# Transposes in a PSUM bank of their own, attention and mLSTM products in the other three: a hybrid decoder block on one core

## The chip, the cores and the metric

The kernel runs on one core of one Trainium2 chip. The metric is the device time of one execution in microseconds (us); the median of several runs counts. Names of engines in the profile: PE is TensorE's matmuls, PEld its weight loads, DVE is VectorE, ACT ScalarE, POOL GpSimd, SP SyncE, which issues all DMAs of this kernel. "L204" is line 204 of the kernel's file.

## What is computed

One decoder block over 2048 tokens of 1024 features, in float32. The reference, cut to what matters here:

```python
h = modulate(rms_norm(x, g_pre_mix), shift_m, scale_m)
proj = h @ w_in        # q,k,v | mLSTM q,k,v,o | pre-gates i,f | branch gates
q_a, k_a = rope(q_a, positions), rope(k_a, positions)      # 8 q heads, 2 kv heads of 64
y_a = sliding_window_attention(q_a, k_a, v_a, sinks)       # blocks of 128, window 128
qk_m = silu(causal_depthwise_conv(concat(q_m, k_m)))
h_m = mlstm_chunkwise(q_m, k_m, v_m, i_pre, f_pre)         # 4 heads of 128
y_m = sigmoid(o_m) * head_layer_norm(h_m)
merged = sigmoid(g_a) * (y_a @ w_branch_attn) + sigmoid(g_m) * (y_m @ w_branch_mlstm)
x = x + gate_m * rms_norm(merged @ w_out, g_post_mix)
h2 = modulate(rms_norm(x, g_pre_ffn), shift_f, scale_f)
ff = (silu(h2 @ w_ffn_gate) * (h2 @ w_ffn_up)) @ w_ffn_down   # 2816 wide
x = x + gate_f * rms_norm(ff, g_post_ffn)
```

## The kernel before

**Precision and products.** A float32 operand is split into two float32r halves, hi (a copy on ACT) and lo (the difference, on DVE: L259 and L260 for weights, L1356 and L1357 for the FFN), and a product is three matmuls: hi by hi, hi by lo, lo by hi. All of them go through mm (L200 to L204); all transposes go through transpose (L206 to L209) and are matmuls with an identity matrix. Where a weight pair allows it, four products of half-size blocks are made from seven (pair_parts).

**Blocks.** Tokens are worked on in four blocks of 512; two make a superblock (function superblock), and the FFN follows with program2 over the same two halves. In a superblock, b0 and b1 are its blocks, and the items come in this order: q and kv projections of b0, attend(b0), the v projection of the mLSTM (vm) of b0, then kv, q and vm of b1, attend(b1), then 14 pairs of column groups for both blocks (in_pair), then the outputs of both.

**PSUM.** There are eight banks, each a tile of 128 x 512 float32. ps_acc has four under the tag acc, for projections (acc_tile). ps_mix has four under the tag mix (mix_tile), for everything else: the transposes of h (hprep, L515), q (q_stream, L767), k (k_stream, L794), gates (gates, L846 and L877), mLSTM k (chunk_state, L1015) and mLSTM output (chunk_out, L1086), the score, probability and output tiles of attention (L921, L954, L966), the mLSTM's products (L1032, L1048, L1059), the transposes of h_combine for the FFN (L1398), and those FFN products that don't go to an acc tile (L1481, L1756).

**SBUF tiles that matter here.** tx is a tag with nine buffers of 128 x 512 float32 (L103). A projected kv or q tile is copied from its acc bank into a tx tile (L806, L781), the rotary writes a second one (L754 to L761), and both are kept until the transposed halves, which overwrite them, have been written to at_d in memory (L773, L799 to L801). at() reads them back for attention (L903 to L908). v of the mLSTM takes a tx tile as well (L826, L827).

**Order.** The projections are a list of parts that run2 goes through. Beside them run generators, the streams: each yields a time after which it is due again, counted by a sum of planned PE time (now), and tick() after every few matmuls takes up what is due. finish(...) runs streams until the ones that it names have ended. That gives the order in which the code asks for tiles and writes instructions down. From it the tile framework makes each engine's own order: it goes by readiness in its own reckoning of time, hands out the buffers of a tag, and sets the semaphores. So an engine's order in the trace differs from the code's in many places. The delays that matter here are L_ROPE and L_ROPEK (after which a rotated q or k tile is transposed), L_HT (between two h tiles), L_SOFT, L_PT and L_PV (in attention) and L_GATE and L_SCAN (in the gates).

**The parts that the change touches.** Transposes of h: one(k) in hprep makes four 128 x 128 transposes into one tile, which ACT reads twice (L518, L520) and DVE makes the lo half (L521); eight such tiles a block. q_stream: four transposes a tile, read by ACT (L771) and DVE (L772). k_stream: one transpose, read by ACT (L797) and DVE (L798), two writes to at_d. Attention on one block of 128 queries: four score tiles (for two halves of the heads and two kv groups), copied by ACT (L931) and masked by DVE (L933); softmax on DVE, ACT and POOL (L938 to L950); two tiles of transposed probabilities (L956, read by L959 and L963); one output tile of four matmuls (L969, read by L972 and L973). Two attention streams alternate, for even and odd blocks.

Of the kernel before, what the change touches and what calls it, by code (L numbers as in the profile page):

```python
# [10 lines left out]
F32 = mybir.dt.float32  # L11
# [8 lines left out]
P = 128  # L20
# [51 lines left out]
def decoder_block(ctx: ExitStack, tc: tile.TileContext, a: dict, out: bass.AP, dbg=None):  # L72
# [24 lines left out]
    def acc_tile():  # L97
        return ps_acc.tile([P, 512], F32, tag="acc", name=nm("acc"))

    def mix_tile():  # L100
        return ps_mix.tile([P, 512], F32, tag="mix", name=nm("mix"))

# [383 lines left out]
    def hprep(b, first=False):  # L486
# [25 lines left out]
        def one(k):  # L512
            name = f"{k // 4 + 1}{odd + 1}"
            hi, lo = (hc_part(name, i)[:, k % 4, :] for i in range(2))
            ps = mix_tile()  # L515
            for t in range(NT):
                transpose(ps[:, t * P:(t + 1) * P], xs[t][:, k * P:(k + 1) * P])
            A.activation(hi, ps, AF.Identity, scale=s1[:, k:k + 1], bias=sh1[:, k:k + 1])  # L518
            v = vs[k // 4][:, k % 4, :]
            A.activation(v, ps, AF.Identity, scale=s1[:, k:k + 1], bias=sh1[:, k:k + 1])  # L520
            (G if first else V).tensor_tensor(lo, v, hi.bitcast(F32), op=ALU.subtract)  # L521
# [214 lines left out]
    def superblock(sb):  # L736
        b0, b1 = 2 * sb, 2 * sb + 1
        R = {}
# [25 lines left out]
        def q_stream(b, t, yz):  # L764
            yield L_ROPE
            y, z = yz
            pt = mix_tile()  # L767
            for j in range(GQ):
                transpose(pt[:, j * P:(j + 1) * P], y[:, j * P:(j + 1) * P])
            hi, lo = z.bitcast(F32R), y.bitcast(F32R)  # L770
            A.activation(hi, pt, AF.Copy, scale=HD ** -0.5)  # L771
            V.scalar_tensor_tensor(lo, pt, HD ** -0.5, hi.bitcast(F32), op0=ALU.mult, op1=ALU.subtract)  # L772
            for i, q in enumerate((hi, lo)):  # L773
                nc.sync.dma_start(at_d[b * NT + t][:, i * 512:(i + 1) * 512], q.bitcast(F32))
# [16 lines left out]
        def k_stream(n, yz):  # L791
            yield L_ROPEK
            y, z = yz
            pt = mix_tile()  # L794
            transpose(pt[:, :P], y)
            kk = z[:, P:3 * P].bitcast(F32R).rearrange("p (i k) -> p i k", i=2)
            A.copy(kk[:, 0, :], pt[:, :P])  # L797
            V.tensor_tensor(kk[:, 1, :], pt[:, :P], kk[:, 0, :].bitcast(F32), op=ALU.subtract)  # L798
            for n_, u in ((n, 1), (n + 1, 0)):  # L799
                if n_ < S // P:  # L800
                    nc.sync.dma_start(at_d[n_][:, AT_K:AT_V].rearrange("p (i u k) -> p i u k", i=2, u=2)[:, :, u, :], kk.bitcast(F32))  # L801
# [30 lines left out]
        def gates(b):  # L832
# [12 lines left out]
            yield L_GATE  # L845
            pg = mix_tile()  # L846
            for t in range(NT):
# [28 lines left out]
            yield L_SCAN  # L876
            pc_ = mix_tile()  # L877
            for t in range(NT):
# [122 lines left out]
        def chunk_state(c):  # L1001
# [12 lines left out]
            yield L_LOAD  # L1014
            pk = mix_tile()  # L1015
            for hh in range(MH):
# [25 lines left out]
        def chunk_out(c):  # L1042
# [42 lines left out]
            yield L_LN  # L1085
            py = mix_tile()  # L1086
            for hh in range(MH):
# [290 lines left out]
    def h_combine(b2, rows, quarters, sums):  # L1378
# [14 lines left out]
        for k in range(4):  # L1393
            xk = xn
            v = {}
            for j, (half, i) in enumerate(QUADS):
                kk = k + 4 * half
                ps = mix_tile()  # L1398
                for t in range(4):
# [66 lines left out]
    def pair_parts(w, c0, done, new, spare, bank):  # L1466

        raw = raw_cols2(w, c0)
        R = {}

        def make(i, prep):
            B = PROD[i][1]

            def mms(wt):
# [13 lines left out]
                combine(i, ps, R, new, done)  # L1488
            return Part(raw, prep, mms, weave=bank is not mix_tile, ahead=4)

# [69 lines left out]
    def gate_up(b2):  # L1560
        late = None
        for p in range(NP):
# [26 lines left out]

            gp, up = (list(pair_parts(w, p * 256, done, unit, unit, mix_tile)) for w, done in ((wg, done_g), (wu, done_u)))  # L1590
            load, sums = down_weights(p)
# [35 lines left out]
    def down(b2):  # L1627
# [105 lines left out]
        def make(raw, i, p, j):  # L1733
# [16 lines left out]
            def mms(ab):  # L1750
                if p == 0:
                    for t in range(NT):
                        if i == 0:
                            R[t]["X"] = acc_tile()
                        if i not in IN_X:
                            R[t]["Y"] = mix_tile()  # L1756
                if hold:
# [112 lines left out]
```

## Time and profile before

| | us |
|---|---|
| median of 3 runs | 2711.97 |
| lowest and highest run | 2708.91, 2712.32 |
| the profiled execution | 2716.59 |
| its span, first to last instruction | 2714.9 |
| PE idle in the span (2714.9 - 2639.2 busy) | 75.7 |

How to read it: all times are in us from the span's start, unless marked ns. A row of groups is line, engine, operation, out<-in by the program's names without buffer numbers, shapes, count, then busy us and mean ns of one, then idle time of the engine just before them with what ended it. A row of the timeline is start, length, engine, line, operation, names, shapes and count, with an idle time in brackets. A row of one tile or one line has the shortest, median and longest duration in ns and the first and last start. Matmuls are pipelined, so the records of one after another overlap, and PE's throughput is read from starts or from busy time over a count.

### The profile page before, as it was taken

How to read it: one execution, taken by the hardware profiler on the slowest of the kernel's cores; microseconds unless marked ns; L12 is line 12 of the kernel's file. 1: busy time of each engine (PE TensorE's matmuls, PEld its weight loads, DVE VectorE, ACT ScalarE, POOL GpSimd, SP SyncE). 2: the span in 40 equal slices, each digit the busy share in tenths (PEclk: the TensorE clock that was granted, in tenths of full speed). 3: DMA queues.
4: the chain of work that ended last, by engine and by line, in shares of the span. 5: the costliest groups of instructions: out<-in, count | busy, mean ns of one | idle time of the engine just before them, and what ended most of it. 6: DMA issues, size and time to landing. Idle time of an engine off the chain costs nothing.

```text
span 2714.9 us, 35793 instructions
## 1 busy us (share of the span) xinstructions
PE 2639.2 (97%) x12310; PEld 2138.9 (79%) x12310; DVE 1986.2 (73%) x3906; ACT 1299.8 (48%) x2558; POOL 148.2 (5%) x189
## 2 busy tenths in 40 slices
PE   6989999999998999999999999999999999999998
PEld 4867788888885678888887888888877888888886
DVE  7968788778695778876687777776677676766456
ACT  5556544444755564444563443335554333333444
POOL 2010001100101000110000000000000000000000
PEclk8999999999998999999999999999999999999999
DMA  7654355897574544678765564436675232324566
GB/s 249 206 184 157 128 172 179 269 340 248 196 235 147 196 138 138 213 231 291 251 224 198 175 201 152 155 113 213 215 271 188 97 117 86 113 97 144 186 210 217
DMA packets 353639, 511.90 MB, mean 189 GB/s; under 512 B 25120, under 2 KB 213660, under 8 KB 348208
## 3 DMA queue, kind: packets, MB, share of 16 engines
q1 hardware_dynamic: 353456, 509.61, 56.9%
q8 instruction: 97, 1.59, 0.2%
q14 instruction: 86, 0.70, 0.1%
HBM read 357.12 MB, written 144.02 MB: 185 GB/s over the span
## 4 chain that ended last, share of the span: by engine, by line
PE 85%; DVE 7%; DMA 4%; ACT 2%; issue 1%; POOL 0%; SPq 0%; DVEq 0%; ACTq 0%; POOLq 0%
PE acc L204 61%; PE mix L204 22%; PE mix L209 2%; DVE hl L1357 1%; DVE tm L428 1%; DMA raw<-as_d 1%; ACT tm L946 1%; ACT hl L1356 1%; DMA raw<-in_w_in_dram 1%; DMA at_d<-tx 0%; DMA big<-in_x_dram 0%; DVE wlo L260 0%; DMA tx<-in_w_ada_dram 0%; DVE w L1667 0%; DMA at<-at_d 0%
## 5 line engine op out<-in xcount | busy, mean ns | idle before, releaser
L204 PE MATMUL acc<-big,hl 128*128 128x512 f32 x3936 | 940.8, 394 | 4.3 <-ACT tx L827 1.8
L204 PEld LDWEIGHTS acc<-big,hl 128*128 128x128 f32 x3936 | 733.3, 188 | 172.5 <-issue 13.8
L1356 ACT CAST hl<-raw 128x512 fp32r<-128x512 f32 x732 | 440.1, 621 | 493.4 <-PE acc L204 222.2
L1357 DVE TENSOR_TENSOR hl<-raw,hl 128x512 fp32r<-128x512 f32 x732 | 496.3, 694 | 194.8 <-ACT hl L1356 194.0
L204 PE MATMUL acc<-whi,big 128*128 128x512 f32 (+1 forms) x1280 | 379.3, 377 | 10.8 <-ACT big L518 8.4
L204 PEld LDWEIGHTS acc<-whi,big 128*128 128x128 f32 x1280 | 236.2, 192 | 52.4 <-ACT big L518 8.5
L204 PE MATMUL mix<-big,hl 128*128 128x512 f32 x1056 | 263.9, 391 | 1.7 <-ACT hl L1356 1.1
L204 PE MATMUL acc<-wlo,big 128*128 128x512 f32 (+1 forms) x640 | 241.2, 379 | 6.4 <-DVE wlo L260 6.4
L204 PE MATMUL acc<-hl,hl 128*128 128x512 f32 x1008 | 237.4, 393 | 5.1 <-DVE hl L1357 3.4
L204 PEld LDWEIGHTS mix<-big,hl 128*128 128x128 f32 x1056 | 197.9, 188 | 45.9 <-ACT hl L1356 1.9
L204 PEld LDWEIGHTS acc<-hl,hl 128*128 128x128 f32 x1008 | 187.0, 188 | 50.9 <-DVE hl L1357 8.8
L204 PE MATMUL mix<-hl,hl 128*128 128x512 f32 x792 | 182.7, 391 | 1.3 <-DVE hl L1357 0.9
L204 PEld LDWEIGHTS mix<-hl,hl 128*128 128x128 f32 x792 | 147.9, 188 | 35.3 <-DVE hl L1357 3.1
L204 PE MATMUL acc<-big,whi 128*128 128x512 f32 x512 | 157.4, 393 | 0.0
L260 DVE TENSOR_TENSOR wlo<-raw,whi 128x1024 fp32r<-128x1024 f32 (+1 forms) x96 | 109.0, 1137 | 65.5 <-ACT whi L259 59.8
L259 ACT CAST whi<-raw 128x1024 fp32r<-128x1024 f32 (+1 forms) x96 | 94.3, 983 | 123.8 <-PE acc L204 110.4
L204 PEld LDWEIGHTS acc<-wlo,big 128*128 128x128 f32 x640 | 123.7, 193 | 28.3 <-DVE wlo L260 8.6
L475 POOL TENSOR_TENSOR rs<-ms,nhalf 128x1 f32<-128x1 f32 (+1 forms) x56 | 42.6, 772 | 1617.5 <-DVE ms L473 1610.5
L204 PE MATMUL mix<-hcT4h,hl 128*128 128x512 f32 x352 | 117.7, 395 | 0.7 <-ACT hl L1356 0.7
L204 PE MATMUL acc<-hcT2h,hl 128*128 128x512 f32 x352 | 117.6, 394 | 0.0
L204 PEld LDWEIGHTS acc<-big,whi 128*128 128x128 f32 x512 | 95.4, 188 | 19.2
L204 PE MATMUL acc<-big,wlo 128*128 128x512 f32 x256 | 97.7, 393 | 0.0
(330 smaller groups left out, 3491.5 us busy)
## 6 DMA issues: line engine op xcount, KB each, us to landing
raw<-in_w_in_dram SPq DMA_DIRECT2D x48, 1024.0 KB
as_d<-w SPq DMA_DIRECT2D x154, 256.0 KB
raw<-as_d SPq DMA_DIRECT2D x70, 512.0 KB
raw<-in_w_ffn_gate_dram SPq DMA_DIRECT2D x22, 1024.0 KB
raw<-in_w_ffn_up_dram SPq DMA_DIRECT2D x22, 1024.0 KB
raw<-ws_d SPq DMA_DIRECT2D x40, 512.0 KB
y_d<-tm SPq DMA_DIRECT2D x64, 256.0 KB
tx<-in_w_ada_dram SPq DMA_DIRECT2D x64, 256.0 KB
```

The source lines that it names most:

```text
L204: T.matmul(o, lhsT=lhsT, rhs=rhs, start=start, stop=stop, skip_group_check=resumed)
L209: T.transpose(o, i, ident[:k, :k])
L259: A.copy(hv, src)
L260: V.tensor_tensor(lv, src, hv.bitcast(F32), op=ALU.subtract)
L428: V.scalar_tensor_tensor(acc, raw[:, k, :], c_, acc, op0=ALU.mult, op1=ALU.add)
L475: G.tensor_tensor(r[:, :n], ms[:, :n], nhalf[:, :n], op=ALU.pow)
L946: A.activation(sc[g][:, j, :], sc[g][:, j, :], AF.Exp, bias=nm_[:, hd:hd + 1], accum_out=sums[:, hd:hd + 1])
L1356: A.copy(v(hi), src)
L1357: V.tensor_tensor(v(lo), src, v(hi).bitcast(F32), op=ALU.subtract)
```

## The change

mix_tile keeps the pool's tag mix, now with three buffers. A new tr_tile has one buffer under the tag tr, and any_tile takes the two in turn: three mix tiles, then one tr tile. The transposes of h, q, k, the gates (twice), mLSTM k and mLSTM output ask for tr_tile; attention's tiles (its transposed probabilities too) and the mLSTM's products still ask for mix_tile; h_combine's transposes and the FFN's products ask for any_tile. The pool has four banks as before. In pair_parts the test for weaving streams into the matmuls now compares with any_tile, so that the FFN's parts stay unwoven.

```diff
--- before.py
+++ after.py
@@ -97,8 +97,17 @@
     def acc_tile():
         return ps_acc.tile([P, 512], F32, tag="acc", name=nm("acc"))
 
+    turn = [0]
+
     def mix_tile():
-        return ps_mix.tile([P, 512], F32, tag="mix", name=nm("mix"))
+        return ps_mix.tile([P, 512], F32, tag="mix", name=nm("mix"), bufs=3)
+
+    def tr_tile():
+        return ps_mix.tile([P, 512], F32, tag="tr", name=nm("tr"), bufs=1)
+
+    def any_tile():
+        turn[0] = (turn[0] + 1) % 4
+        return mix_tile() if turn[0] else tr_tile()
 
     def tx(shape, dtype=F32):
         return tpool.tile(shape, dtype, tag="tx", name=nm("tx"), bufs=9)
@@ -512,7 +521,7 @@
         def one(k):
             name = f"{k // 4 + 1}{odd + 1}"
             hi, lo = (hc_part(name, i)[:, k % 4, :] for i in range(2))
-            ps = mix_tile()
+            ps = tr_tile()
             for t in range(NT):
                 transpose(ps[:, t * P:(t + 1) * P], xs[t][:, k * P:(k + 1) * P])
             A.activation(hi, ps, AF.Identity, scale=s1[:, k:k + 1], bias=sh1[:, k:k + 1])
@@ -764,7 +773,7 @@
         def q_stream(b, t, yz):
             yield L_ROPE
             y, z = yz
-            pt = mix_tile()
+            pt = tr_tile()
             for j in range(GQ):
                 transpose(pt[:, j * P:(j + 1) * P], y[:, j * P:(j + 1) * P])
             hi, lo = z.bitcast(F32R), y.bitcast(F32R)
@@ -791,7 +800,7 @@
         def k_stream(n, yz):
             yield L_ROPEK
             y, z = yz
-            pt = mix_tile()
+            pt = tr_tile()
             transpose(pt[:, :P], y)
             kk = z[:, P:3 * P].bitcast(F32R).rearrange("p (i k) -> p i k", i=2)
             A.copy(kk[:, 0, :], pt[:, :P])
@@ -843,7 +852,7 @@
             V.tensor_tensor(l_, l_, d_, op=ALU.add)
             V.scalar_tensor_tensor(fv, fv, 0.0, l_, op0=ALU.min, op1=ALU.subtract)
             yield L_GATE
-            pg = mix_tile()
+            pg = tr_tile()
             for t in range(NT):
                 transpose(pg[:36, t * P:(t + 1) * P], gt[:, t, :])
             lf = tm([MH, TB])
@@ -874,7 +883,7 @@
             mp = small.tile([P, MH, 8], F32, tag="mp", name=nm("mp"), bufs=2)
             nc.sync.dma_start(mp, sm_d.unsqueeze(0).to_broadcast([P, MH, 8]))
             yield L_SCAN
-            pc_ = mix_tile()
+            pc_ = tr_tile()
             for t in range(NT):
                 transpose(pc_[:, t * 68:(t + 1) * 68], rw[:, t * P:(t + 1) * P])
             cl = small.tile([P, NT, 3, 4], F32, tag="cl", name=nm("cl"), bufs=2)
@@ -1012,7 +1021,7 @@
             vc = vmt[n_ % 2]
             nc.sync.dma_start(vc[:, :, :MD], vm_d[b][:, t, :].rearrange("p (h d) -> p h d", h=MH))
             yield L_LOAD
-            pk = mix_tile()
+            pk = tr_tile()
             for hh in range(MH):
                 transpose(pk[:, hh * P:(hh + 1) * P], km[:, hh, :])
             kw = tm([P, MH, P])
@@ -1083,7 +1092,7 @@
                 o = pn[hh // 2][:, (hh % 2) * 129:(hh % 2) * 129 + P]
                 A.activation(ym[:, hh, :], o, AF.Identity, scale=cf[:, hh:hh + 1], bias=vr[:, hh:hh + 1])
             yield L_LN
-            py = mix_tile()
+            py = tr_tile()
             for hh in range(MH):
                 transpose(py[:, hh * P:(hh + 1) * P], ym[:, hh, :])
             V.tensor_tensor(om, py.rearrange("p (h t) -> p h t", h=MH), om, op=ALU.mult)
@@ -1395,7 +1404,7 @@
             v = {}
             for j, (half, i) in enumerate(QUADS):
                 kk = k + 4 * half
-                ps = mix_tile()
+                ps = any_tile()
                 for t in range(4):
                     transpose(ps[:, t * P:(t + 1) * P], xk[j][:, t, :])
                 q = quarters()
@@ -1486,7 +1495,7 @@
                     mm(ps, l[1], r[0], False, kk == 3, True)
                     yield
                 combine(i, ps, R, new, done)
-            return Part(raw, prep, mms, weave=bank is not mix_tile, ahead=4)
+            return Part(raw, prep, mms, weave=bank is not any_tile, ahead=4)
 
         for i, prep in enumerate(a_operands(raw, spare)):
             yield make(i, prep)
@@ -1587,7 +1596,7 @@
                 for n, t_ in (("S1", s1_), ("S3", a_["21"]), ("S2", s2_), ("S4", s4_)):
                     nc.sync.dma_start(as_d[b2][:, IDX[n], p, :], t_)
 
-            gp, up = (list(pair_parts(w, p * 256, done, unit, unit, mix_tile)) for w, done in ((wg, done_g), (wu, done_u)))
+            gp, up = (list(pair_parts(w, p * 256, done, unit, unit, any_tile)) for w, done in ((wg, done_g), (wu, done_u)))
             load, sums = down_weights(p)
             if F.get("late") is not None and p == 0:
                 def a_step():
@@ -1753,7 +1762,7 @@
                         if i == 0:
                             R[t]["X"] = acc_tile()
                         if i not in IN_X:
-                            R[t]["Y"] = mix_tile()
+                            R[t]["Y"] = any_tile()
                 if hold:
                     F.setdefault("held", []).append((p, ab))
                     if p == NP - 1:
```

## The prediction

> **What bounds the kernel now.** I read the page first, then PE's busy time by stretches, then who read which tile in the stretches where PE is not full.
>
> ```profile
> span 2714.9 us, 35793 instructions
> ## 1 busy us (share of the span) xinstructions
> PE 2639.2 (97%) x12310; PEld 2138.9 (79%) x12310; DVE 1986.2 (73%) x3906; ACT 1299.8 (48%) x2558; POOL 148.2 (5%) x189
> ```
>
> PE is busy for 97% of the span, so all that any change of waits can win lies in 76 us. The view of windows says where they are (columns: stretch and length, then busy us and count of PE, PEld, DVE, ACT and POOL, then PE's granted clock, DMA share, GB/s):
>
> ```profile
> 158.50:184.50 26.00, 19.14 (x97) 9.61 (x96) 13.38 (x38) 14.67 (x53) 4.68 (x5) 0.87 0.39 119
> 838.00:866.40 28.40, 18.98 (x88) 9.82 (x84) 13.77 (x39) 14.56 (x52) 4.67 (x5) 0.70 0.35 113
> 210.00:310.00 100.00, 100.00 (x476) 72.53 (x474) 78.38 (x171) 63.12 (x163) 9.36 (x8) 1.00 0.39 126
> 890.00:935.00 45.00, 40.50 (x199) 31.72 (x200) 35.19 (x84) 31.58 (x85) 4.16 (x4) 0.96 0.55 178
> 66.00:120.00 54.00, 49.41 (x311) 44.12 (x310) 50.47 (x126) 33.94 (x59) 1.17 (x2) 0.98 0.65 209
> 745.00:800.00 55.00, 49.73 (x310) 43.89 (x311) 48.95 (x131) 28.80 (x52) 0.00 (x0) 0.97 0.75 248
> 1440.00:1840.00 400.00, 400.00 (x1757) 328.18 (x1756) 299.17 (x489) 154.04 (x280) 2.16 (x4) 1.00 0.51 163
> ```
>
> In two stretches, 158.5 to 184.5 and 838 to 866.4, PE is a quarter to a third idle although no other engine is near full. Attention woven into projection matmuls doesn't do that by itself: from 210 to 310 it leaves PE no idle time. The two stretches are the same place of the program in the two superblocks: the q projection of the second block has ended and its v projection should run. What it lacks is shown by ACT's reads and writes of the tx tiles from 120 to 200, and by the last step of the rotary on DVE (L761) in two windows:
>
> ```profile
> L781 ACT COPY tx<-acc x4: 585/586/592, 153.2 to 187.0; 128x512 f32<-128x512 f32 x4
> L797 ACT CAST tx<-mix x4: 265/269/272, 182.4 to 186.3; 128x128 fp32r<-128x128 f32 x4
> L771 ACT ACTIVATE tx<-mix x4: 585/591/597, 188.1 to 195.8; 128x512 fp32r<-128x512 f32 x4
> ...
>   DMA at_d<-tx: 1.0, 2
> ```
> ```profile
> 120.00:137.00 17.00, 0.86 (x4) 0.97 0.59 187
> 137.00:181.80 44.80, 0.00 (x0) 0.93 0.44 134
> ```
>
> The four rotated key tiles were ready by 137, but their transposes were read (L797) from 182.4 on, 45 us later. Until then they kept their tx tiles (two for each key tile, of nine in all), so of the four copies of q out of the acc banks (L781) one ran at 153.2 and the others by 187.0, behind a DMA of those tx tiles to at_d. Three acc banks stood full, v had one, and PE was left with attention alone. In the second superblock the last q copies and the key reads fall together again, at 863.6 to 868.3:
>
> ```profile
> L781 ACT COPY tx<-acc x4: 592/593/607, 827.0 to 868.3; 128x512 f32<-128x512 f32 x4
> L797 ACT CAST tx<-mix x4: 265/266/272, 863.6 to 868.2; 128x128 fp32r<-128x128 f32 x4
> ```
>
> Why were the key transposes late? All tiles of the tag mix come in the order in which the code asks for them, and the code asks for the tiles of some attention blocks just ahead of the key tile's. Those wait for softmax; the key tile waits behind them for no reason of its own. That order is my reading of these rows, and the forecast hangs on it.
>
> **The change part by part.** *Keys, queries, gates, h, k and y of the mLSTM go to a bank of their own.* For keys this takes the queue behind attention away. Ahead of them in the new queue stand only gate transposes, which don't wait for attention. So the key transposes run near 137, their two at_d writes a tile go to SP's queue some 45 us earlier, the tx tiles come free, q is copied out as it ends, and v runs while attention is woven in. The gain is each stretch less the time that its PE work needs. The work, by form, for the first stretch, then for the second, then the transposes of both:
>
> ```profile
> L204 PE MATMUL mix<-tm,at 128*64 128x512 f32 x22 | 9.9, 800 | 0.0
> L204 PE MATMUL mix<-at 64*128 64x256 f32 x48 | 4.4, 289 | 2.7 <-DMA at<-at_d 2.7
> ```
> ```profile
> L204 PE MATMUL mix<-tm,at 128*64 128x512 f32 x20 | 9.7, 898 | 0.0
> L204 PE MATMUL mix<-at 64*128 64x256 f32 x48 | 5.7, 415 | 3.7 <-DMA at<-at_d 2.4 <-DVE tm L933 1.3
> ```
> ```profile
> 158.50:184.50 26.00, 3.78 (x19) 2.30 (x19) 0.87 0.39 119
> 838.00:866.40 28.40, 4.29 (x19) 2.65 (x19) 0.70 0.35 113
> ```
>
> What is left of 97 and 88 instructions is 8 and 1 projection matmuls. The prices come from other places: the whole run's group of the 128*64 matmuls, and single rows of PE's timeline.
>
> ```profile
> L204 PE MATMUL mix<-tm,at 128*64 128x512 f32 x124 | 51.7, 695 | 0.0
> ```
> ```profile
> 74.92 0.60 PE L209 MATMUL mix<-ident,tx 128*128 128x128 f32 x4
> ...
> 108.87 0.28 PE L204 MATMUL acc<-wlo,big 128*128 128x264 f32 x1
> ...
> 149.48 1.07 PE L204 MATMUL mix<-tm,at 128*64 128x512 f32 x2
> ...
> 753.05 0.60 PE L209 MATMUL mix<-ident,tx 128*128 128x128 f32 x4
> ...
> 784.20 0.37 PE L204 MATMUL acc<-whi,big 128*128 128x264 f32 x1
> ...
> 836.71 1.94 PE L204 MATMUL mix<-tm,at 128*64 128x512 f32 x8
> ```
>
> One 128*64 matmul takes 0.42 on the whole (51.7/124), 0.24 at best (1.94/8) and 0.53 in a lone pair (1.07/2). A score matmul takes 0.09 (4.4/48), a transpose 0.13 (0.60/4 less an end that overlaps), a projection matmul 0.23 (400/1757). First stretch: 22x0.42 + 48x0.09 + 19x0.13 + 8x0.23 = 17.9 of 26.0, so 8.1 to win; with 0.24 it is 12.0, with 0.53 it is 5.7. Second: 20x0.42 + 4.3 + 2.5 + 0.2 = 15.4 of 28.4, so 13.0; bounds 16.6 and 10.8. Together 21.1, between 16.5 and 28.6; I take the whole run's pace since woven attention has that pace. Later, 890 to 935 holds 4.5 us of PE idle in which late v copies have a part; I take 1.5 of it, between 0 and 4.5.
>
> *The price: one bank for transposes.* A tile's next transposes now wait until the last tile is read. The nearest rows are those of the start of the first superblock, 65.9 to 91.7, ACT's two reads of an h tile in that window, and DVE's read of the q tile whose transposes began at 74.92:
>
> ```profile
> L518 ACT ACTIVATE big<-mix,sh,s 128x512 fp32r<-128x512 f32 x8 | 6.4, 799 | 3.7 <-PE mix L209 3.7
> L520 ACT ACTIVATE big<-mix,sh,s 128x512 f32<-128x512 f32 x8 | 6.4, 796 | 0.0
> ```
> ```profile
> 80.91 0.69 DVE L772 SCALAR_TENSOR_TENSOR tx<-mix,tx 128x512 fp32r<-128x512 f32 x1
> ```
>
> Alone an h tile takes 0.6 + 0.8 + 0.8 = 2.2, a q tile 0.6 + 0.6 + 0.7 = 1.9; the slow bound is the q tile of these rows, which waited for a full DVE (50.47 of 54.00): 80.91 + 0.69 - 74.92 = 6.7. Twelve such tiles (8 h, 4 q) now run four deep; in series they need 25 to 80 us from 66 on. Their last users are the kv matmuls of the second block: these begin at 108.87, and need the last quarter of h about 7 us later (48 matmuls of 0.12 to 0.15), so at 116; that leaves 50 us, or 4.2 a tile. I take 3.2 a tile, nearer the fast end because DVE's delay was DVE's own queue, which a single bank doesn't lengthen: 104, and PE doesn't wait. In the second superblock nine tiles from 753.05 have until 791 (784.20 + 7), again 4.2 a tile. For ACT and DVE work that comes in another order I put 1 us for each of these two starts (bounds -2, where DVE gets to the weights' halves sooner, and +4). In the first 66 us the h tiles come in pairs, and the second of a pair waits for one more 0.6 and a handover, 0.7 four times at most; I put 1.5 (0 to 2.8).
>
> *Attention and mLSTM products rotate over three banks.* Of a block's four score tiles the fourth waits until the first is read, at most one 0.59 copy and one 0.69 read by DVE: 0 to 1.3 for each of 16 blocks, 0 to 20. What hides it is the projection matmuls that stand between (210 to 310: no idle time in 100 us), so I take 0.2, in all 3. If that cover were gone PE itself would wait. The mLSTM's five product tiles a chunk run under pair matmuls that don't use this pool; 0.
>
> *any_tile* gives three mix tiles and one tr in turn, so the four banks of the FFN and of h's combination rotate as before: 0, in a phase that leaves PE no idle time (1440 to 1840, 400.00 of 400).
>
> Sum: -21.1 - 1.5 + 1.5 + 2 + 3 = -16.1. The profiled execution took 2716.59 (its span and 1.7 around it), which gives 2700.5 for its like; the runs' median, 2711.97, is 4.6 lower, so 2695.9: **2696**.
>
> **The rivals.** *All of it is won*: the single bank and the three cost nothing, each of the two starts wins 1, and 890 to 935 keeps no idle time: 21.1 + 2 + 4.5 = 27.6, so 2684. For it: ACT at 63 of 100 has room. Against: DVE at 78 of 100, which gets denser as the stalls go. *The wait moves to attention*: the fourth score tile costs 1.0 in each block, because PE's records come in one order and a score matmul that waits holds the projections behind it: 16 in place of 3, so 2709. For it: in the second stretch PE already waits 1.3 for DVE's read of a score tile (L933, above). Here belongs also that the keys still wait, behind late gate transposes in the new tag. *The single bank is too slow*, and the kernel gets slower: at 5.5 us a tile the twelve end at 66 + 66 = 132, 16 late, the nine at 802.5, 11.5 late; with the gains (22.6 less 4.5) 2712 - 18.1 + 27.5 = 2721. It decides from 4.2 a tile on; for it speaks DVE's 93% in that stretch, against it the 25 us that the tiles need alone. The Trainium skill has a rule on this side: in Perfetto Trace Analysis, under Optimizing Tensor Performance, Matmuls, it asks that independent groups rotate through different PSUM banks, so that evacuating one overlaps the next one's matmuls. For the transposes the change does the contrary; no row of this trace shows one bank alone, and by that rule this rival would be the forecast.
>
> **How the numbers follow.** The forecast has 0.58 with a range of its own of 2686 to 2707; all of it 0.13; the moved wait 0.13; the slow bank 0.16. The range 2680 to 2720 holds the first three and leaves the last out. A measurement of this kernel tells some 0.2%, 5.4 us, from no change: faster is the first two, 0.70 with a little of the forecast's own tail gone; within that, the moved wait and that tail, 0.14; slower 0.16.
>
> **What would show it.** Right: L797 of the second block near 137, not 182; the four L781 copies within some 5 us; no stretch like 838 to 866 in the windows; PE's idle time down by about 16. Wrong: L797 still behind attention (the order was misread); PE waiting at the 128x264 matmuls for h (the slow bank); PE idle at score matmuls for DVE L933 in many blocks (three banks). FFN stretches that change by more than 2 us would show that I misread any_tile.

## The result, and the profile after: 26 us slower

The changed kernel takes 2738.52 us (median of 4 runs, 2737.57 to 2739.17) and the kernel before 2712.14 beside it: ratio 1.0100, interval 1.0087 to 1.0112. The forecast was 2696, some 16 us faster. Measured again (e9) the ratio was 1.0106 (1.0091 to 1.0121).

The top of the page after:

```profile
span 2737.5 us, 35776 instructions
## 1 busy us (share of the span) xinstructions
PE 2653.5 (97%) x12310; PEld 2143.3 (78%) x12310; DVE 1990.1 (73%) x3906; ACT 1302.7 (48%) x2558; POOL 152.4 (6%) x189
```

The span is 22.6 longer. (The profiled run of before was itself above the median of its runs, so the medians stand further apart.) PE's busy time grew by 14.3 with the same 12310 matmuls, its idle time by 8.3: part of the loss shows as slower matmuls, so idle time alone would hide more than half. Line numbers after are those of before plus 9. First the window of 0 to 66 in the kernel before, then windows of the kernel after (columns as in the prediction):

```profile
0.00:66.00 66.00, 41.13 (x179) 30.37 (x180) 48.05 (x137) 34.49 (x68) 16.22 (x55) 0.90 0.72 256
```
```profile
0.00:66.00 66.00, 38.93 (x167) 27.40 (x167) 47.17 (x137) 33.68 (x66) 16.34 (x54) 0.90 0.73 256
66.00:120.00 54.00, 45.59 (x245) 38.62 (x246) 39.21 (x98) 26.02 (x40) 3.11 (x3) 0.91 0.39 124
158.50:184.50 26.00, 22.32 (x95) 14.70 (x94) 18.42 (x62) 15.36 (x53) 4.54 (x4) 0.93 0.53 169
838.00:866.40 28.40, 28.40 (x135) 21.07 (x134) 22.65 (x89) 20.27 (x61) 4.64 (x4) 1.00 0.47 142
1463.00:1862.50 399.50, 399.50 (x1755) 327.73 (x1754) 298.60 (x488) 153.65 (x279) 2.16 (x4) 1.00 0.51 163
```

The two stalls shrank, one of them to nothing. That is no effect of the delay: in windows moved on with it, 170.4 to 196.4 and 853 to 881.4, PE idles 2.2 and 0. But 66 to 120 lost what they gave: 245 matmuls in place of 311. Where the time goes is read best from one row that both kernels have at the end of each stage. First the kernel before, then after: ACT's copies of the first block's q (L781, L790) and v (L827, L836), its reading of the first superblock's output (L596, L605), and ACT's rows at the first FFN pair.

```profile
L781 ACT COPY tx<-acc x4: 605/613/627, 65.9 to 67.3; 128x512 f32<-128x512 f32 x4
L827 ACT COPY tx<-acc x4: 578/586/587, 105.4 to 109.3; 128x512 f32<-128x512 f32 x4
L596 ACT ACTIVATE big<-acc x4: 585/598/599, 601.3 to 605.4; 128x512 f32<-128x512 f32 x4
1428.51 0.62 ACT L1356 CAST hl<-raw 128x512 fp32r<-128x512 f32 x1 [3.38 <-PE acc L204]
1429.03 0.58 ACT L1497 COPY w<-acc 128x512 f32<-128x512 f32 x1
```
```profile
L790 ACT COPY tx<-acc x4: 581/608/633, 70.6 to 73.4; 128x512 f32<-128x512 f32 x4
L836 ACT COPY tx<-acc x4: 583/586/606, 117.3 to 125.1; 128x512 f32<-128x512 f32 x4
L605 ACT ACTIVATE big<-acc x4: 591/598/599, 614.6 to 618.7; 128x512 f32<-128x512 f32 x4
1445.92 0.62 ACT L1365 CAST hl<-raw 128x512 fp32r<-128x512 f32 x1 [3.38 <-PE acc L213]
1452.52 0.58 ACT L1506 COPY w<-acc 128x512 f32<-128x512 f32 x1 [5.98 <-DMA x<-tm]
```

The changed kernel is late by 4.7 at 66, by 11.9 at 105, by 13.3 after the first superblock, by 17.4 after the second; then one copy waits 6.0 for a DMA, and 22.6 is left at the end. So the loss comes in four pieces: the first 66 us, the start of the second block (66 to 120), the same place of the second superblock, and one wait at the FFN's first pair that the prediction didn't foresee.

The second piece is the single bank. The view of single lines shows h's transposes on PE, ACT's reads of them, and ACT's reads of all eight key tiles (count, then shortest, median and longest ns, then first and last start):

```profile
L218 PE MATMUL tr<-ident,big x32: 271/272/330, 67.9 to 121.1; 128*128 128x128 f32 x32
L527 ACT ACTIVATE big<-tr,sh,s x8: 772/778/808, 69.3 to 121.4; 128x512 fp32r<-128x512 f32 x8
L806 ACT CAST tx<-tr x8: 254/265/283, 125.0 to 179.9; 128x128 fp32r<-128x128 f32 x8
```

Twelve tiles, eight of h and four of q, take from 67.9 to the last read at 122.9: 55.0 us, 4.58 a tile. Following each tile in the timeline, 32.0 us of them are holding (first transpose to end of the last read, 2.67 a tile) and 23.0 are eleven pauses from a read's end to the next tile's first transpose. The pauses are 2.1 in the mean, but uneven: four of them, 3.4 to 6.4 long, make 17.7. The timeline of some q and h tiles shows what both are made of (start, duration, engine, line, operation, and in brackets the idle time before it and what ended it):

```profile
77.67 0.60 PE L218 MATMUL tr<-ident,tx 128*128 128x128 f32 x4
78.31 0.60 ACT L780 ACTIVATE tx<-tr 128x512 fp32r<-128x512 f32 x1
...
83.42 0.68 DVE L781 SCALAR_TENSOR_TENSOR tx<-tr,tx 128x512 fp32r<-128x512 f32 x1
...
87.87 0.60 PE L218 MATMUL tr<-ident,big 128*128 128x128 f32 x4
...
95.19 0.60 PE L218 MATMUL tr<-ident,tx 128*128 128x128 f32 x4
95.82 0.60 ACT L780 ACTIVATE tx<-tr 128x512 fp32r<-128x512 f32 x1 [4.16 <-PE tr L218]
...
100.25 0.38 ACT L815 COPY tx<-acc 128x264 f32<-128x264 f32 x1 [1.76 <-DMA at_d<-tx]
...
100.68 0.80 PE L213 MATMUL acc<-whi,big 128*128 128x512 f32 x1 [2.83 <-ACT tx L815]
```

The tile of 77.67 is read by ACT at once, but by DVE only at 83.42: its own queue is long. Until 84.1 nobody else can use the bank. It is free then, but the next tile's transposes come at 87.87, because they have a fixed place in PE's order and projection matmuls stand before it: from 84.1 to 87.87 PE has no idle time. And what is late in the end is not h: at 95.82 ACT has waited 4.16 for a q tile, behind it in ACT's order stands the copy of kv out of an acc bank (L815), that copy waits for a tx tile whose DMA to at_d still runs, and PE waits 2.83 for the copy. Behind this wait the 128x512 matmuls last 0.63 up to 103.83 and 0.39 from 105.37 on, and the granted clock from 95 to 106 is 0.69: this is how a wait comes back as busy time. In the view of waits over the whole run (us, times, longest) the wait for these copies is PE's largest:

```profile
PE acc L213 <- ACT tx L815: 9.3, 4, 3.5
```

Only 2.8 of the 9.3 fall between 66 and 130. PE's largest wait there is 3.0 for the lo half of the weights (L269), but the kernel before has 2.6 of the same kind (L260), and none for the kv copies.

### The profile page after: what moved, and what is told of

Read it like the earlier page. It is cut to its first block, busy times and chain, and to the rows that moved or that the text cites. A ratio compares the mean times of both kernels' runs of the same rounds, so it can differ in the third digit from the quotient of the medians.

```text
span 2737.5 us, 35776 instructions
## 1 busy us (share of the span) xinstructions
PE 2653.5 (97%) x12310; PEld 2143.3 (78%) x12310; DVE 1990.1 (73%) x3906; ACT 1302.7 (48%) x2558; POOL 152.4 (6%) x189
## 4 chain that ended last, share of the span: by engine, by line
PE 83%; DVE 4%; DMA 4%; ACT 2%; issue 1%; POOL 0%; SPq 0%; POOLq 0%; DVEq 0%; ACTq 0%
PE acc L213 59%; PE mix L213 18%; PE tr L213 4%; DVE hl L1366 1%; PE tr L218 1%; PE mix L218 1%; DMA at_d<-tx 1%; DMA raw<-as_d 1%; ACT hl L1365 0%; DMA tm<-negm_d 0%; DMA big<-g_d 0%; DMA x<-tm 0%; DVE big L1366 0%; DMA at<-at_d 0%; DMA x1n<-tm 0%
## 5 line engine op out<-in xcount | busy, mean ns | idle before, releaser
L213 PEld LDWEIGHTS acc<-big,hl 128*128 128x128 f32 x3936 | 731.3, 188 | 171.3 <-issue 16.1
L213 PE MATMUL acc<-whi,big 128*128 128x512 f32 (+1 forms) x1280 | 388.5, 382 | 22.8 <-ACT tx L815 9.3
L213 PEld LDWEIGHTS acc<-whi,big 128*128 128x128 f32 x1280 | 238.4, 194 | 69.7 <-ACT tx L815 10.2
L213 PE MATMUL mix<-big,hl 128*128 128x512 f32 x792 | 198.0, 391 | 1.2 <-DVE hl L1366 0.7
L213 PEld LDWEIGHTS mix<-big,hl 128*128 128x128 f32 x792 | 148.3, 188 | 33.9 <-DVE hl L1366 1.3
L269 DVE TENSOR_TENSOR wlo<-raw,whi 128x1024 fp32r<-128x1024 f32 (+1 forms) x96 | 109.7, 1145 | 72.4 <-ACT whi L268 66.3
L213 PE MATMUL mix<-hl,hl 128*128 128x512 f32 x594 | 158.3, 391 | 1.4 <-DVE ms L482 0.9
L213 PEld LDWEIGHTS mix<-hl,hl 128*128 128x128 f32 x594 | 110.9, 188 | 27.5 <-DVE hl L1366 3.0
L213 PE MATMUL mix<-hcT4h,hl 128*128 128x512 f32 x264 | 88.3, 395 | 0.8 <-ACT hl L1365 0.8
```

Source lines behind the costliest of these rows:

```text
L213: T.matmul(o, lhsT=lhsT, rhs=rhs, start=start, stop=stop, skip_group_check=resumed)
L269: V.tensor_tensor(lv, src, hv.bitcast(F32), op=ALU.subtract)
```

## The experiments

The kernels ran beside the kernel before; times are medians, differences are against the kernel before on the same chip, and ratios have 95% intervals. Except e11 each is an edit of the changed kernel.

### Which tiles pay

**e1: only the keys (and the FFN's turn) keep the own bank.**

```diff
 hprep, q_stream, gates (2), chunk_state, chunk_out:
-    ... = tr_tile()
+    ... = mix_tile()
```

> Only the key tiles (and one FFN tile in four) use the bank of their own; h, q, gates, k and y of the mLSTM go back to the tag mix, which keeps three banks. Theory 'one queue' (the single bank is too slow for h and q: 12 tiles took 67.9 to 122.9, of which about 23 us were pauses between the release of a tile and the next tile's first transpose): with h and q on three rotating banks most of the loss of the two superblocks' starts, 4 + 9 + 4 us, goes, and the keys are free of attention, so 2695 to 2710. Theory 'three banks' (the loss is attention's and the mLSTM's lost bank): it stays at 2725 to 2740. Theory 'FFN turn' (the 5 us lost at the first FFN pair come from any_tile): 5 us at 1440 to 1460 remain in either case.

2705.91, 4.3 faster than before (0.9985, 0.9975 to 0.9994). The keys of the second block are read from 141.8 on, 40 us earlier than before, and PE no longer idles in either stretch:

```profile
L806 ACT CAST tx<-tr x4: 247/268/274, 141.8 to 163.0; 128x128 fp32r<-128x128 f32 x4
158.50:184.50 26.00, 26.00 (x137) 19.02 (x137) 17.28 (x41) 14.03 (x38) 2.08 (x2) 1.00 0.68 228
838.00:866.40 28.40, 28.40 (x141) 20.15 (x140) 19.51 (x44) 15.49 (x40) 2.08 (x2) 1.00 0.79 251
```

So the prediction's reading of the keys holds: freed from attention's order, the keys come early and the stalls leave these windows. A part of the waiting only moves on: from 140 to 200 PE still idles 3.7 (6.9 before), from 800 to 900 it idles 3.8 (12.5 before).

**e2: no own bank, the mixers share three.** All seven `tr_tile()` calls of the mixers become `mix_tile()`.

> All mixer tiles share the tag mix with three banks; the fourth bank is used only by the FFN's turn. So a bank is taken away and nothing gets an own one. One queue: 2712 to 2720, the stalls of before (keys behind attention) are there again, and h's last tile of the second block is near 90, not 122. Three banks: 2730 to 2740, with waits at score tiles.

2720.27, 10.0 slower (1.0033, 1.002 to 1.0046), 0.3 beyond what the first theory allowed. The stall at 838 is back in part, and the keys of the second block are read late again:

```profile
L806 ACT CAST tx<-mix x4: 265/269/298, 184.0 to 190.7; 128x128 fp32r<-128x128 f32 x4
838.00:866.40 28.40, 24.46 (x117) 15.67 (x117) 13.35 (x30) 12.90 (x38) 2.08 (x2) 0.84 0.52 156
```

A lost bank costs 10, and the keys' own bank is worth 14.4 (e2 less e1). The first is more than the prediction charged, the second less than it hoped for; together they would still make the kernel faster.

**e3: two banks for the transposes, two for the products** (`bufs=2` for both tags, the turn over two).

> Two banks for the transposes' tag, two for attention and mLSTM products, FFN in turn over both. One queue: the pause between two tiles lies beside the other tile's reading, twelve tiles end near 100, not 122, so the starts lose nothing, and attention pays: 2700 to 2720. Three banks: with two banks attention's price is at least double what it is in the changed kernel, 2740 to 2770.

2721.96, 11.7 slower (1.0042, 1.0027 to 1.0057): 15 less than the single bank loses, although attention has only two banks left. "Three banks" falls with it; the first theory's range is missed by 2 us. The h tiles are read from 71.5 to 104.1, not to 121.4:

```profile
L527 ACT ACTIVATE big<-tr,sh,s x8: 777/782/798, 71.5 to 104.1; 128x512 fp32r<-128x512 f32 x8
```

**e4: all tiles, the mixers' too, in turn over the two names** (every `mix_tile()` and `tr_tile()` becomes `any_tile()`): four banks, as before.

> Every tile of the pool, the mixers' too, is taken in turn from mix, mix, mix, tr: four banks in call order as before, only with two names. One queue and three banks both say 2712 within 5. FFN turn says 5 more, at 1440 to 1460, because the FFN's tiles are those of the changed kernel.

2714.88, 4.7 slower (1.0014, 1.0004 to 1.0023). There is no extra wait at the FFN, so the turn there costs nothing. It also gives a measure: the same four banks under two names, in a strict turn, move the time by some 5 us, presumably through another order of instructions. A difference of that size between two of these kernels is put down to an edit only where a row of the trace shows it.

**e5, e6, e7: h and q back, h back, q back** (the named tiles to `mix_tile()`, all others in the own bank).

> From the changed kernel, only h and q go back to the three banks; keys, gates, k and y of the mLSTM keep the single bank. One queue: the loss of the starts is h's and q's, so nearly all of the difference to the keys alone (2706) goes: 2702 to 2712, with h's last tile of the second block near 90 and its keys near 140 to 165. If gates or the mLSTM's k and y carry a part of the loss, 2715 to 2725, with keys of the second block later than 165.

2709.83, 2.2 less than before (0.9993, 0.9984 to 1.0002: no difference is shown). The keys of the second block are read from 141.6 to 156.3. Gates and the mLSTM's tiles in the own bank cost little: 2 more than the keys alone, within the measure of e4.

> From the changed kernel, only h goes back. In the single bank stay q, keys, gates, k, y. One queue, where the chain is what costs and each tile has a price of some 4.6 us: eight tiles fewer between 66 and 123, the kv projection of the second block begins near 109, not 121; 2705 to 2718. If it is q's wait for the rotary on DVE that blocks the line and not the number of tiles, little is won: 2720 to 2735.

2723.76, 11.7 slower (1.0046, 1.0031 to 1.0061). Eight tiles fewer in the line, and 11.7 of 26 to 28 are still lost. The time lies in the expectation's second case, though more is won than "little". The v copies of the first block come at 123.6, later than in the changed kernel, while h is done early:

```profile
L527 ACT ACTIVATE big<-mix,sh,s x8: 777/814/860, 71.2 to 82.0; 128x512 fp32r<-128x512 f32 x8
L836 ACT COPY tx<-acc x4: 582/587/588, 123.6 to 128.1; 128x512 f32<-128x512 f32 x4
```

> From the changed kernel, only q goes back; h, keys, gates, k, y stay in the single bank. By the number of tiles (4.6 us each) the eight h tiles end near 67 + 8 x 4.6 = 104, before the 116 at which the second block's kv needs them: 2708 to 2720. If q's wait for DVE holds the line, the h tiles run at 2.2 to 3.5 and end by 95, and the time is that of the kernel with both back, 2702 to 2712. If h alone is enough to be late, 2722 to 2738, kv of the second block beginning after 112.

2715.15, 3.1 slower (1.0015, 1.0006 to 1.0025): the time of the expectation's first case, with h as early as in its second. Without q in the line the eight h tiles are read from 69.7 to 93.5, 28 us sooner than with it. What h alone costs beside e5, 5.3 us, is had by 66: the window of 0 to 66 has 167 matmuls here and in the changed kernel, where the kernel before has 179. It is h's and nothing else's: the first block's q copies (L790) begin at 70.4 to 71.0 in every kernel with h in the single bank (the changed one, e7, e10, e13) and at 64.9 to 66.5 in all the others.

```profile
L527 ACT ACTIVATE big<-tr,sh,s x8: 769/780/804, 69.7 to 93.5; 128x512 fp32r<-128x512 f32 x8
0.00:66.00 66.00, 38.12 (x167) 26.61 (x168) 47.17 (x137) 33.76 (x66) 16.65 (x54) 0.92 0.73 256
```

So h in the single bank costs 5, q costs 14 (e6 less e5), and both together more than the sum. Where they cost it is shown by the reading of the first superblock's output in e5, e6 and e7:

```profile
L605 ACT ACTIVATE big<-acc x4: 590/598/600, 600.7 to 604.8; 128x512 f32<-128x512 f32 x4
L605 ACT ACTIVATE big<-acc x4: 590/598/600, 616.8 to 620.9; 128x512 f32<-128x512 f32 x4
L605 ACT ACTIVATE big<-acc x4: 589/594/600, 604.6 to 608.7; 128x512 f32<-128x512 f32 x4
```

Beside e5, q alone loses 16.1 in the first superblock and h alone 3.9, and both together (614.6, 611.2 and 610.1 in the changed kernel, e9 and e13) no more than q alone. From this row to the same row of the second superblock it takes 689.0 in e5, 683.7 with q alone and 686.1 with h alone, but 696.5, 699.0 and 697.6 with both. So what goes beyond the sum is lost in the second superblock, and why it needs both there was not tested.

### What q's late tiles hold

In the kernel before, the first block's four q tiles are transposed from 74.92 on and read by 84.6; in e6, through one bank, it takes until 108.2, 8.3 a tile. The last read before, then the first transposes and the last read in e6:

```profile
83.31 1.28 DVE L772 SCALAR_TENSOR_TENSOR tx<-mix,tx 128x512 fp32r<-128x512 f32 x2
```
```profile
75.14 0.60 PE L218 MATMUL tr<-ident,tx 128*128 128x128 f32 x4
107.47 0.69 DVE L781 SCALAR_TENSOR_TENSOR tx<-tr,tx 128x512 fp32r<-128x512 f32 x1 [0.64 <-ACT tx L780]
```

The waits of ACT and of PE in e6, from 66 to 130, show two candidates. ACT's order: ACT waits 8.8 for q tiles, with the kv copies behind them. And the tx tiles: a copy waits 4.6 for the DMA that frees one.

```profile
ACT tx L780 <- PE tr L218: 8.8, 2, 7.1
...
ACT tx L815 <- DMA at_d<-tx: 4.6, 1, 4.6
```
```profile
PE acc L213 <- ACT tx L815: 8.1, 3, 5.7
```

**e14: e6 with q's first read on DVE**, so that ACT never waits for a q tile.

```diff
-            A.activation(hi, pt, AF.Copy, scale=HD ** -0.5)
+            V.tensor_scalar(hi, pt, HD ** -0.5, None, op0=ALU.mult)
```

> The kernel with h back and q in the single bank (2724), with q's first read of the tile on DVE in place of ACT. Theory 'ACT order' (ACT waited 8.8 us for q's transposes with the kv copies behind it, and PE 8.1 us for these copies): PE's wait for the kv copies between 66 and 130 falls below 3 us, 2710 to 2719. Theory 'line' (the order of the single bank alone): PE waits as long as before, for DVE or for the copies, 2721 to 2732, since DVE has 16 more operations of 0.7 us in its fullest stretches.

2729.58, 20.1 slower (1.0076, 1.0061 to 1.0091). The edit also gives DVE 16 more operations of 0.7 us, so a part of the 8.4 more than e6 may be DVE's own. But "ACT order" falls: with ACT free, the kv copies wait for tx itself, and PE waits as long as before.

```profile
ACT tx L815 <- DMA at_d<-tx: 14.2, 2, 13.3
```
```profile
PE acc L213 <- ACT tx L815: 7.8, 3, 5.7
PE tr L218 <- DVE tx L781: 3.7, 2, 2.7
```

**e17: e14 with ten tx tiles and eight tm tiles** (nine and nine before).

> The kernel with h back and q's first read on DVE (2730), with ten tx tiles and eight tm tiles. Theory 'tx': the kv copies no longer stand behind ACT's reads of q, so one tx tile more lets a copy go: their wait for the DMA at_d<-tx (14.2 us between 66 and 130) at least halves, PE's wait for them (7.8) falls below 4, and the time falls by more than the 9 us that the exchange wins in the kernel before, to 2720 or less. Theory 'line': 2720 to 2730, with PE's waits there as they are.

2722.95, 12.6 slower (1.0048, 1.0033 to 1.0064): 7.5 less than e14, but the same exchange wins 9.2 in the kernel before (e11). The wait for the DMA is gone, PE's wait for the copies fell to 2.2 as "tx" expected, and the time did not follow, because the waits took other names:

```profile
ACT tx L815 <- DVE tx L781: 10.1, 1, 10.1
```
```profile
PE tr L218 <- DVE tx L781: 4.4, 2, 4.0
PE acc L213 <- DVE wlo L269: 4.1, 2, 3.6
PE acc L213 <- ACT tx L815: 2.2, 1, 2.2
```

**e10 and e11: the same exchange in the changed kernel and in the kernel before.**

> The changed kernel with ten tx tiles and eight tm tiles in place of nine and nine (there is no room for more of both). Theory 'tx' (q tiles in the line of the single bank keep their tx tiles, the copies of kv out of the acc banks wait for one, PE waits for the copies): PE's wait for the kv copies (4.4 us from 66 to 140, 9.3 in all) shrinks and the time falls by 5 to 15 us, more than the same exchange changes the kernel before. Theory 'PE order' (the loss is the pauses of the line itself): the same as the exchange does to the kernel before, within 4.

> The same exchange in the kernel before, as the control: its q copies of the second block wait for tx tiles too (158 to 184, 838 to 866), so both theories allow a gain of 0 to 10 us; attention has a tm tile less, which may take it back.

e10: 2730.05, 20.5 slower than before (1.008, 1.0065 to 1.0095), so 7.3 won against the changed kernel beside it (e9); e11: 2700.41, 9.2 faster than before (0.9966, 0.9954 to 0.9978). The changed kernel gains no more than its control, and most of its gain is the FFN's wait of 6 (next), which this edit happens to remove. "Tx" as the one cause falls. Late q tiles hold the bank, ACT's order and tx at once; take away one of these holds and the next one shows. What is common to e6, e14 and e17 is the line: a q tile read late by a full DVE (busy 14.00 of the 14 us from 76 to 90 in all three), and the next tile behind it. That the line is the cause is what is left over; no run makes DVE read these tiles early in a single bank.

### The 6 us at the FFN's first pair

**e9: the changed kernel again.**

> The changed kernel once more, beside the kernel before on the same chip. If the 5 us at the first FFN pair (1441 to 1453, a copy into w that waits for the DMA x<-tm) belong to this program, its profile shows them again and the median is 2738 +- 2; if they belong to that one execution or chip, they are gone and it is 2731 to 2735.

2737.38 (1.0106), and the wait is there again, 6.1 long: it belongs to this program. `w`, the FFN's first tile, is put where a tm tile of the mixers was. The addresses in the two programs (bytes within a partition):

```text
             first w    last two row tiles of the mixers (tm)
before       161792     159744, 167936
changed      161792     157696, 161792
```

**e13: one of the two last row tiles comes from tx.**

```diff
-            xr = (tm if late and t == NT - 1 else tx)([P, 512])
+            xr = (tm if late and t == NT - 1 and c.start else tx)([P, 512])
```

> The changed kernel with one of its two last row tiles of the mixers taken from tx in place of tm, so that the first FFN tile w lies on memory that has long been free. Theory 'memory': ACT's 6 us wait of the copy into w for the DMA x<-tm is gone, 2731 to 2734 (the changed kernel 2738). If the DMA is late for another reason, 2736 to 2740 with the wait in its place.

2732.12 (1.0083, 1.0069 to 1.0097), 22.6 slower than the kernel before, where the changed kernel was 26.4 and 27.8 slower: 4 to 5 us back. ACT no longer waits for a DMA there: from the reading of the second superblock's output to the first copy into `w` it takes 135.6, where the changed kernel took 141.4 and 141.7 (e9) and the kernel before 135.4. So this piece is not the banks' turn: with another order in which tiles came free, the last row tile, whose DMA still runs, had come to lie under the first `w`.

### A version that beats both

**e8 and e18: only the keys in the own bank, four tiles side by side in one tile; h and the mLSTM in turn over all four banks.**

```diff
+            if n % NT == 0:
+                R["kt"] = tr_tile()
-            pt = tr_tile()
+            pt = R["kt"][:, n % NT * P:(n % NT + 1) * P]
 ...
 hprep, chunk_state, chunk_out (transposes and products):
-    ... = tr_tile() or mix_tile()
+    ... = any_tile()
 q_stream, gates (2):
-    ... = tr_tile()
+    ... = mix_tile()
```

> Only the keys use the bank of their own, and the four key tiles of a block lie side by side in one tile of it, so no key waits for the reading of the one before it; h and the mLSTM's tiles take all four banks in turn. From the kernel with keys alone (2706): the four key reads of the second block come within 10 us, not 20, and the mLSTM's phase loses nothing for the third bank (there the kernel with three banks lost 5 us between 437 and 670). One queue and this reading of the lost bank together: 2694 to 2703. If the remaining cost is attention's on three banks or the later merging of attention into the projections, it stays at 2704 to 2710.

> The keys side by side in one tile of their own bank, h and mLSTM in turn over four banks, once more with five rounds: 2700 to 2704, some 8 to 10 us below the kernel before, as in its first measurement; if that was the chip's or the hour's, 2704 to 2708.

2701.86 (0.9964, 0.9951 to 0.9977) and 2697.88 (0.9954, 0.9941 to 0.9966): 10 and 12 faster than before, the best of all, and the second time better than was expected. The tiles that share the keys' bank in turn are called at other times, h ahead of the keys and the mLSTM behind them, so neither stands in a key's way. From the second measurement:

```profile
span 2693.5 us, 35779 instructions
```
```profile
L808 ACT CAST tx<-tr x4: 249/268/272, 133.6 to 153.2; 128x128 fp32r<-128x128 f32 x4
```

The expectation of four reads within 10 us was wrong; they still spread over 20. **e16**, the keys side by side without the turn, tells why that didn't matter:

> Only the keys in the own bank, four side by side in one tile; h and mLSTM stay on three banks. If the handover between the key tiles was what e1 still lost, 2700 to 2704; if e8's gain came from the four banks for h and mLSTM, 2704 to 2708.

2705.42 (0.9984, 0.9975 to 0.9993), the same as e1, with reads from 142.1 to 162.8. The handover between key tiles is not what spreads them; e8 gains 6 to 8 on e16 by the four banks for h and mLSTM, and which of the two gains it was not separated.

**e12: e8 with the second block's attention in the turn too; e15: e8 with ten tx tiles.**

> The keys alone in the own bank, side by side in one tile, h and mLSTM in turn over four banks, and now also the attention of the second block of each superblock, behind whose call no key tile comes. If what is left of the lost bank's price is attention's, 3 to 6 us below the version without it (2702): 2695 to 2699. If not, 2700 to 2704.

> The keys alone in the own bank, side by side in one tile, h and mLSTM in turn over four banks (2702 without more), and ten tx tiles with eight tm tiles (the kernel before gained 9 by that). If the two gains are of different waits they add: 2690 to 2696. If both are the same stretches of waiting for tx, no better than either: 2698 to 2703.

e12: 2705.56 (0.9982, 0.9973 to 0.9992). e15: 2703.29 (0.998, 0.997 to 0.9989). Neither adds to e8. For e15, which lies 0.3 above that range, it speaks for the expectation's second case, that both gains are of the same stretches of waiting; e12 missed both of its cases, and why it is worse than e8 was not followed up.

## Why the prediction was wrong, point by point

**The key step was right, but not in this kernel.** Keys were late because of the order of calls behind attention; e1 shows it, with most of the stalls gone and 14.4 us between e1 and e2, where the sum had 21.1 + 1.5. In the changed kernel the second block's keys are read late as well, the last at 179.9, not near 137, since in their new bank they stand behind everything else that is late. The prediction had written this down among the rivals, for gates alone, at 2709.

**The step that failed: the price of the single bank.** The sum charged 1 us for each of the two starts; e13 less e5 puts h and q in that bank at 25. Two choices were wrong. First, 3.2 a tile "because DVE's delay was DVE's own queue, which a single bank doesn't lengthen". The bank indeed doesn't lengthen DVE's queue (the first q tile is held 6.4, and was 6.7 before), but it makes everyone behind the tile wait for it: four banks hide a reader that is 5 us late, one bank passes it on to all tiles after it. The measured tile takes 4.58, beyond the deciding point of 4.2 that the prediction itself had worked out. Its pauses, 2.1 in the mean, were charged nothing; they come from PE's fixed order, in which a tile's transposes can't start when the bank comes free but only when their turn comes. Second, the deadline was put at h's last user, at 116. q's users came sooner: a q tile holds two of nine tx tiles, and kv copies wait for these and stand behind q in ACT's order. e7, with h alone, ends h at 93.5 and loses 5; e6, with q alone, has read h by 82 and loses 14. This is the very chain that the prediction had found for the keys (tile late, tx held, acc bank full, PE waits), and it was not asked of q. How the 25 divides between the chain's links stays open, as does why the second superblock loses only with both kinds in the bank.

**The first 66 us**: 1.5 charged with 2.8 as the bound, 4.7 at L790 and 5.3 by e7 less e5. Mis-sized: the five h tiles from 47.21 on start 3.4 to 5.5 apart (47.21, 50.91, 56.37, 59.79, 64.11), so none comes as a close second of a pair; in e5, with three banks, eight transposes still run in a row at 55.96.

**Three banks**: 3 charged, 10 measured in e2, within the bounds of 0 to 20. Mis-sized; mLSTM's share was taken as 0; e8 against e16 shows that h and mLSTM together pay some of it.

**any_tile**: 0, and right: 399.50 of 399.5 in the FFN. But the sign given for a misreading ("FFN stretches that change by more than 2 us") would have misled: the FFN's first pair lost 6 us through memory, not through banks.

**The rivals**: the single bank that is too slow, 2721, is what happened, with the right deciding point and too small a price; it had 0.16. The Trainium skill's rule that it named (Perfetto Trace Analysis, Optimizing Tensor Performance, Matmuls: independent groups should rotate through different PSUM banks) agrees with the runs: with a second bank for the transposes the loss falls from 26 to 12, e3.

The ledger, each line against the kernel before or the kernel named: a bank lost 10.0 (e2); keys' own bank -14.4 (e1 less e2); gates, k and y in it 2.1 (e5); h 5.3 (e7 less e5); q 13.9 (e6 less e5); h and q in one line, beyond their sum, 5.6 (e13 less the rest); the FFN's memory 4 to 5. The sum, 26 to 28, is that of the two measurements by construction, since the sixth term is the remainder. The terms of 2.1 and 5.6 are no larger than e4's measure, and no single row stands for them; the 5.3 has the late q copies at 66 behind it.

## What to carry to other kernels

A buffer of its own frees a tile from its neighbours' order only if everything else that shares that buffer is quick; give it to the one tile that is stuck, not to all tiles of its kind. Before a rotation of four is cut to one, take for each tile the time from its first write to its last read at the slowest reader, add the pause until the in-order engine comes round again, and ask what the tile's holder keeps meanwhile (input buffers, its readers' queues), not only who needs its result. The stall that a change removes tells which resource was scarce; look whether the change makes another tile hold the same resource.

## What the runs showed of the hardware that was not expected

PE's idle time understates a loss: of 22.6 us, 14.3 came as busy time of the same 12310 matmuls, as in the stretch from 95 to 106, where the granted clock was 0.69 behind a wait. And memory that one pool gave back was not free for the next until its last DMA had landed: a copy with nothing else to wait for stood 5.98 us in one profile of the changed kernel and 6.1 in the other, where no other kernel waited more than 2.9 for that DMA; which of nine buffers the last tile got decided it.
